# Conformer layer: six of eight convolution tiles on TensorE and two on VectorE, TensorE's order fixed from the second group of products on, two modulation vectors placed behind the convolution

## The chip, the core and the metric

One core of a Trainium2 chip runs the whole network in one launch. The metric is device time in microseconds (us), from the first to the last instruction with what the runtime adds around it; lower is better. The engines are TensorE (PE: matrix products; PEld is its weight load), VectorE (DVE), ScalarE (ACT), GpSimd (POOL), and SyncE (SP), whose queue issues nearly all DMA transfers, strictly in the order in which they stand there.

## The reference

Four layers over 256 latent tokens and 256 context tokens of 1024 features, in float32. Layers 0 and 3 mix tokens by attention, layer 1 by a Conformer convolution, layer 2 by a short convolution; each layer ends in an MLP. Every layer is modulated by six vectors, products of a conditioning vector with `mod_w[layer]` (1024 x 6144):

```python
def conformer_conv(h, w1, b1, dw, dwb, ln_g, ln_b, w2, b2):
    u = h @ w1 + b1
    a, g = jnp.split(u, 2, axis=-1)
    u = a * jax.nn.sigmoid(g)
    u = dwconv(u, dw) + dwb            # 31 taps along the tokens, each feature by itself
    u = jax.nn.silu(layernorm(u, ln_g, ln_b))
    return u @ w2 + b2

mod_l = (silu_c @ mod_w[i] + mod_b[i]).reshape(b, N_MOD, 1, D_MODEL)     # 0..5
a_l = modulate(rmsnorm(x, norm1_g[i]), mod_l[:, 0], mod_l[:, 1])
x = x + mod_l[:, 2] * y_l                                                # y_l: the mixer's output
m_l = modulate(rmsnorm(x, norm2_g[i]), mod_l[:, 3], mod_l[:, 4])
x = x + mod_l[:, 5] * sq_relu_mlp(m_l, mlp_w1[i], mlp_w2[i])
```

## The kernel before

Activations lie with features on the 128 partitions: eight tiles (j = 0 to 7) of 512 columns, 256 of the latent stream (s = 0) and 256 of the context (s = 1). A float32 product is three TensorE products of high and low halves (`mm3`, lines 105 to 107). Weights come by SP into four `raw` buffers (line 94, 512 KB each) and are split by ScalarE (line 221) and VectorE (line 222) into ten `w` buffers, five pairs.

**The Conformer** runs the first product `h @ w1` in four groups g, each giving tiles j = 2g and 2g+1: group 0 and group 3 by stream (`gemm_turns`, 256 columns at a time), groups 1 and 2 over 512 columns (`gemm`). VectorE forms the gated tile (`out`, line 1004). The 31 taps of a tile are then summed in one of two ways. `conv_vector` is a chain of 31 VectorE operations, handed out a few at a time by `run_some`. `conv_tensor` is 32 TensorE products for one stream or for both, four per tap group on four quarters of the columns of the array; the profile lists two records for each. It needs the tile written to DRAM and read back four times in shifted form (`shifted`, the `mem` and `u4` tiles, on SP) and a tile of tap weights built by VectorE (`tap_weights`). Before, VectorE has tiles 0, 1, 3 and the latent half of 5, and TensorE has 2, 4, 6, 7 and the other half of 5. `layer_norm(s)` follows for each stream: means by products with `ones_d`, squares, `rstd_newton`, `spread`, and the outputs `z`, which the second product (`cv_w2`, in `project`) reads.

**Modulation vectors** are made in two ways too. `mod_vectors` multiplies and adds on VectorE from 256 KB pieces (`mraw`, line 308); it is put in the background of a layer's MLP and steps at a given rate each time the MLP calls `tick`. `mod_tensor` makes a vector by 16 products on TensorE (line 371, two records each) from eight 512 KB pieces that pass through the same four `raw` buffers (issued at line 360), then a copy by ScalarE and four small products (line 380). `need(layer, m)` writes out what is missing of vector m at that place of the program.

**Order.** A scheduler places each engine's instructions by its own estimate, except where `manual_schedule` names an engine, whose instructions then stand as written. Before, this holds for TensorE in the block that begins at the first `self.need(layer, 3)` of `conformer`:

```python
with self.tc.manual_schedule(engines={mybir.EngineType.PE}):
    self.need(layer, 3)
    for j in (4, 6, 7):
        conv_tensor(j, slice(0, 1))
    lat = layer_norm(0)
    self.need(layer, 4)
    ...
```

The vectors of layer 1 are scheduled at line 1304 and after, in layer 0's MLP: 0 and 1, then 2, by `mod_vectors`; 3, 4 and 5 by `mod_tensor` at rate 0, so that they are made where `need` asks for them.

Of the kernel before, what the change touches and what calls it, by code (L numbers as in the profile page):

```python
# [13 lines left out]
ALU = mybir.AluOpType  # L14
# [5 lines left out]
LAT = 256  # L20
# [5 lines left out]
CONF_K = 31  # L26
CONF_PAD = 15
PITCH = 288
VECTOR_TILES = (0, 1, 3)
NEG = -1e30  # L30


class Net:
# [884 lines left out]
    def conformer(self, layer, slot, then):  # L918
        nc, t = self.nc, self.t
# [3 lines left out]
        conv = [None] * KT  # L923
        sig = {}
        two = lambda ap: ap.rearrange("p (s n) -> p s n", s=2)
        on_vector = []
        loaded = self.conv_taps(slot)
        next(loaded)

        def conv_vector(j, u, st):  # L930

            y = two(conv[j])[:, st]
            ys = [y, two(self.hid())[:, st] if j == 5 else y]
            tap = lambda i: self.par("cv_dw", i * KT + j)
            for i in range(CONF_K):
                if i == 0 or i == 1 and j == 5:
                    nc.vector.tensor_scalar(out=ys[i], in0=u[:, st, i:i + LAT], scalar1=tap(i),
                                            scalar2=None if i else self.par("cv_dwb", j), op0=ALU.mult,
                                            op1=ALU.bypass if i else ALU.add)
                else:  # L940
                    nc.vector.scalar_tensor_tensor(out=ys[i % 2], in0=u[:, st, i:i + LAT], scalar=tap(i), in1=ys[i % 2],  # L941
                                                   op0=ALU.mult, op1=ALU.add)
                yield 1
            if j == 5:
                nc.vector.tensor_tensor(out=y, in0=ys[0], in1=ys[1], op=ALU.add)

        def tap_weights(j):

# [33 lines left out]
        def run_some(n):  # L982

            while n and on_vector:
                g = on_vector.pop(0)
                if next(g, 0):
                    on_vector.append(g)
                    n -= 1

        u4, tapw, mem = {}, {}, {}  # L990
        glu = {}
        for g in range(4):
            def out(d, src, c, g=g):
# [13 lines left out]
                if j == 5:  # L1007
                    shifted(j, slice(1, 2))
                    conv[j] = self.hid()
                    on_vector.append(conv_vector(j, glu[j], slice(0, 1)))  # L1010
                    next(on_vector[-1])
                elif j not in VECTOR_TILES:
                    shifted(j, slice(c.start // LAT, c.stop // LAT))
                elif c.stop == NTOK:
                    conv[j] = self.hid()
                    on_vector.append(conv_vector(j, glu[j], slice(0, 2)))
                    next(on_vector[-1])
            segs = [(D + g * LAT, LAT), (g * LAT, LAT)]
            if g == 0:
                self.gemm_turns(self.chunk_pair(w1, segs), acts, out, first=True)  # L1020
            elif g < 3:
                for i, _ in enumerate(self.gemm(w1, segs, acts, cols, out)):
                    run_some(4)
                    if g == 1 and i == 1:
                        taps, mask = next(loaded)
                    if g == 1 and i == 4:
                        for j in (2, 4):
                            tapw[j] = tap_weights(j)
                    if g == 2 and i == 5:
                        conv[2] = self.hid()  # L1030
                        conv_tensor(2, slice(0, 2))
                        tapw[5] = tap_weights(5)
            else:
                self.gemm_turns(self.chunk_pair(w1, segs), acts, out)
                for j in (6, 7):
                    tapw[j] = tap_weights(j)
        for n, j in enumerate((4, 6, 7)):
# [9 lines left out]
        def layer_norm(s):  # L1047

            c = slice(s * LAT, (s + 1) * LAT)
            mean = self.ps()  # L1050
            added = [(4, 6), (4, 5, 6)][s]
            for j in added:
                nc.vector.tensor_tensor(out=total[:, c], in0=total[:, c], in1=conv[j][:, c], op=ALU.add)
            parts = [total] + [conv[j] for j in (4, 6, 7, 5) if j not in added]
            for n, part in enumerate(parts):
                nc.tensor.matmul(out=mean[:, :LAT], lhsT=self.ones_d, rhs=part[:, c], start=n == 0, stop=n == len(parts) - 1)
            for j in range(KT):
# [11 lines left out]
                self.split(y, z[k][0][:, c], z[k][1][:, c])  # L1069
            yield  # L1070

        with self.tc.manual_schedule(engines={mybir.EngineType.PE}):
            self.need(layer, 3)
            for j in (4, 6, 7):
                conv_tensor(j, slice(0, 1))
            lat = layer_norm(0)
            self.need(layer, 4)
            next(lat)
            for j in (4, 5):
                conv_tensor(j, slice(1, 2))  # L1080
# [204 lines left out]
    def run(self, out):  # L1285
# [5 lines left out]
        for layer in range(DEPTH):  # L1291
# [9 lines left out]
            else:  # L1301
                self.short_conv(layer, slot, mixer_end)
            if layer < DEPTH - 1:
                for vectors, rate in (([0, 1], 0.3), ([2], 0.3)) if layer == 0 else (([0, 1], 0.42), ([2], 0.42), ([3, 4], 0.42),
                                                                                   ([5], 0.25)):
# [46 lines left out]
```

## Time and profile before

| what | value |
|---|---|
| time, median of 3 runs | 2265.07 us (2263.01 to 2267.22) |
| the profiled execution's own time | 2267.25 us |
| its span, first to last instruction | 2265.5 us |
| TensorE busy | 2183.5 us (96%) |
| VectorE busy | 1529.6 us (68%) |
| mean granted TensorE clock | 0.982 of full speed |

Times inside the profile run from the span's start; the Conformer's stage lies at about 701 to 976 us. What lies around the span in the profiled execution is 2267.25 - 2265.5 = 1.75 us. Busy shares are means over stages that have different limits, so a change to one stage has to be read from that stage.

### The profile page before, as it was taken

What the parts mean: (1) busy time and instruction counts of PE and PEld (TensorE: products, weight loads), DVE (VectorE), ACT (ScalarE), POOL (GpSimd) and SP (SyncE); (2) the same over time, 40 slices, a digit from 0 to 9 for tenths busy, and PEclk for the clock granted to TensorE, in tenths of its full rate; (3) what the DMA queues carried; (4) which work ended last, traced back from release to release, by engine and by line L of the source; (5) the groups of instructions that cost most, each with busy time, mean ns of one, the idle gap of its engine ahead of it and who ended that gap; (6) DMA issues with size and microseconds to landing.
All of it is one profiled execution on the core that took longest, in us unless ns stands there. A gap on an engine that the chain in (4) does not pass through costs nothing.

```text
span 2265.5 us, 32711 instructions
## 1 busy us (share of the span) xinstructions
PE 2183.5 (96%) x12706; PEld 1789.6 (79%) x12706; DVE 1529.6 (68%) x2684; ACT 867.3 (38%) x1452; POOL 94.5 (4%) x167
## 2 busy tenths in 40 slices
PE   8999999999999848999999999999999999999998
PEld 5766678888889633888888898898888888778998
DVE  5365668585757962797777887579766557677665
ACT  4355544233233101652332332243323234666543
POOL 1112100000000000000000000000000000230000
PEclk9999999999999978999999999999999999999999
DMA  9565545453422255245455534325555425554653
GB/s 320 139 108 76 126 138 162 127 168 98 144 94 77 89 147 199 87 138 176 137 161 167 163 124 133 102 83 176 170 168 181 143 86 177 77 81 138 195 186 128
DMA packets 201308, 316.51 MB, mean 140 GB/s; under 512 B 13797, under 2 KB 68641, under 8 KB 201152
## 3 DMA queue, kind: packets, MB, share of 16 engines
q1 hardware_dynamic: 197232, 307.69, 43.1%
q0 software_dynamic: 3616, 6.60, 4.8%
q8 instruction: 100, 1.64, 0.3%
q14 instruction: 56, 0.46, 0.1%
q10 hardware_dynamic: 304, 0.12, 0.0%
HBM read 311.99 MB, written 2.38 MB: 139 GB/s over the span
## 4 chain that ended last, share of the span: by engine, by line
PE 89%; DVE 4%; issue 3%; DMA 3%; ACT 1%; POOL 0%; ACTq 0%; SPq 0%; POOLq 0%; DVEq 0%
PE mm L105 26%; PE mm L107 26%; PE mm L106 26%; PE mm L745 2%; PE x L735 2%; PE mm L978 2%; PE mm L707 1%; DVE h L941 1%; PE x L371 1%; PE mm L706 1%; DMA e<-in_na_rpb_dram 1%; DMA raw<-in_mod_w_dram 1%; DVE w L222 1%; DMA raw<-in_mlp_w_dram 0%; PE x L527 0%
## 5 line engine op out<-in xcount | busy, mean ns | idle before, releaser
L221 ACT ACTIVATE w<-raw 128x1024 fp32r<-128x1024 f32 (+1 forms) x377 | 392.7, 1054 | 672.1 <-PE mm L106 583.0
L222 DVE TENSOR_TENSOR w<-raw,w 128x1024 fp32r<-128x1024 f32 (+1 forms) x377 | 454.3, 1219 | 286.3 <-ACT w L221 285.2
L105 PE MATMUL mm<-a,w 128*128 128x512 f32 (+2 forms) x1792 | 630.5, 352 | 2.3 <-DVE t L629 1.4
L106 PE MATMUL mm<-a,w 128*128 128x512 f32 (+2 forms) x1792 | 627.3, 351 | 0.0
L107 PE MATMUL mm<-a,w 128*128 128x512 f32 (+2 forms) x1792 | 624.2, 350 | 1.1 <-DVE w L222 1.1
L106 PE MATMUL mm<-h,w 128*128 128x256 f32 (+1 forms) x1504 | 506.2, 337 | 0.4 <-DVE h L222 0.3
L105 PE MATMUL mm<-h,w 128*128 128x512 f32 (+1 forms) x1376 | 472.3, 343 | 0.0
L107 PE MATMUL mm<-h,w 128*128 128x512 f32 (+1 forms) x1376 | 469.8, 342 | 0.0
L105 PEld LDWEIGHTS mm<-a,w 128*128 128x128 f32 x1792 | 337.9, 189 | 54.0 <-issue 4.8
L107 PEld LDWEIGHTS mm<-a,w 128*128 128x128 f32 x1792 | 338.0, 189 | 51.0 <-DVE h L941 2.5
L106 PEld LDWEIGHTS mm<-a,w 128*128 128x128 f32 x1792 | 338.7, 189 | 45.7
L106 PEld LDWEIGHTS mm<-h,w 128*128 128x128 f32 x1504 | 283.8, 189 | 32.4 <-DVE h L222 0.8
L105 PEld LDWEIGHTS mm<-h,w 128*128 128x128 f32 x1376 | 259.0, 188 | 36.3 <-issue 3.9
L107 PEld LDWEIGHTS mm<-h,w 128*128 128x128 f32 x1376 | 259.0, 188 | 33.1 <-DVE mm L713 0.6
L316 DVE SCALAR_TENSOR_TENSOR macc<-mraw,cw,macc 128x512 f32<-128x512 f32 x364 | 255.1, 747 | 13.0 <-DMA mraw<-in_mod_w_dram 12.0
L588 DVE SCALAR_TENSOR_TENSOR x<-mm,mod,x 128x256 f32<-128x256 f32 x288 | 127.4, 479 | 97.8 <-PE mm L107 97.3
L221 ACT ACTIVATE h<-t 128x512 fp32r<-128x512 f32 (+1 forms) x148 | 81.0, 548 | 98.8 <-DVE t L619 85.6
L619 DVE SCALAR_TENSOR_TENSOR t<-mm,t 128x512 f32<-128x512 f32 (+1 forms) x136 | 79.3, 586 | 38.7 <-ACT t L618 38.3
L222 DVE TENSOR_TENSOR h<-t,h 128x512 fp32r<-128x512 f32 (+1 forms) x148 | 86.3, 583 | 25.1 <-ACT h L221 24.6
L618 ACT ACTIVATE t<-mm 128x512 f32<-128x512 f32 (+1 forms) x136 | 69.2, 511 | 85.8 <-PE mm L107 84.6
L371 PE MATMUL x<-raw,cw 128*32 128x512 f32 x224 | 44.8, 673 | 41.4 <-DMA raw<-in_mod_w_dram 41.3
L556 ACT ACTIVATE a<-t,mod 128x256 fp32r<-128x256 f32 x120 | 53.4, 501 | 59.3 <-DVE t L543 59.3
(177 smaller groups left out, 1834.7 us busy)
## 6 DMA issues: line engine op xcount, KB each, us to landing
raw<-in_mlp_w_dram SPq DMA_DIRECT2D x256, 512.0 KB
mraw<-in_mod_w_dram SPq DMA_DIRECT2D x240, 256.0 KB
raw<-in_mod_w_dram SPq DMA_DIRECT2D x56, 512.0 KB
raw<-in_na_wqkv_dram SPq DMA_DIRECT2D x64, 256.0 KB
raw<-in_sc_win_dram SPq DMA_DIRECT2D x24, 512.0 KB
h<-in_mod_w_dram SPq DMA_DIRECT2D x32, 256.0 KB
raw<-in_na_wqkv_dram SPq DMA_DIRECT2D x16, 512.0 KB
raw<-in_na_wo_dram SPq DMA_DIRECT2D x16, 512.0 KB
```

What stands on the lines that cost most here:

```text
L105: mm(out=out, lhsT=a[0], rhs=b[0], start=start, stop=False)
L106: mm(out=out, lhsT=a[0], rhs=b[1], start=False, stop=False)
L107: mm(out=out, lhsT=a[1], rhs=b[0], start=False, stop=stop)
L221: self.nc.scalar.activation(out=hi, in_=src, func=AF.Copy)
L222: self.nc.vector.tensor_tensor(out=lo, in0=src, in1=hi.bitcast(F32), op=ALU.subtract)
L316: nc.vector.scalar_tensor_tensor(out=acc[s], in0=raw, scalar=c, in1=acc[s], op0=ALU.mult, op1=ALU.add)
L371: nc.tensor.matmul(out=ps[32 * g:32 * g + 32], lhsT=self.cw[:, 4 * k0 + g, 2 - 2 * r:34 - 2 * r], rhs=tiles[g], start=n == 0, stop=n == 3, ...
L556: self.nc.scalar.activation(out=hi[:, c], in_=t, func=AF.Identity, bias=sh)
L588: self.nc.vector.scalar_tensor_tensor(out=x, in0=src[:, o:o + LAT], scalar=self.mod1(layer, m, s, j), in1=x, op0=ALU.mult, op1=ALU.add)
L618: nc.scalar.activation(out=r, in_=src, func=AF.Relu)
L619: nc.vector.scalar_tensor_tensor(out=h, in0=src, scalar=0.0, in1=r, op0=ALU.max, op1=ALU.mult)
L735: nc.tensor.transpose(out=tp[:, dst * P:(dst + 1) * P], in_=p[:, j * P:(j + 1) * P], identity=self.ident)
```

## The change

VectorE keeps tiles 0 and 1 whole. TensorE gets tiles 2 to 7 whole, each stream: tiles 2 and 3 before group 3, the others behind it. The means are one product for the VectorE-made total (tiles 0 to 3) and one for each of tiles 4 to 7. TensorE stands as written from the end of group 0 to the means of the second stream. Of layer 1's vectors, 0 to 3 are made by `mod_vectors` in layer 0's MLP (pairs at rate 0.55), and 4 and 5 by `mod_tensor` behind the second stream's means.

```diff
-VECTOR_TILES = (0, 1, 3)
+VECTOR_TILES = (0, 1)
...
+        in_order = ExitStack()
...
-                if j == 5:
-                    shifted(j, slice(1, 2))
-                    conv[j] = self.hid()
-                    on_vector.append(conv_vector(j, glu[j], slice(0, 1)))
-                    next(on_vector[-1])
-                elif j not in VECTOR_TILES:
+                if j not in VECTOR_TILES:
                     shifted(j, slice(c.start // LAT, c.stop // LAT))
...
             if g == 0:
                 self.gemm_turns(self.chunk_pair(w1, segs), acts, out, first=True)
+                in_order.enter_context(self.tc.manual_schedule(engines={mybir.EngineType.PE}))
             elif g < 3:
                 for i, _ in enumerate(self.gemm(w1, segs, acts, cols, out)):
-                    run_some(4)
+                    run_some(3)
                     if g == 1 and i == 1:
                         taps, mask = next(loaded)
-                    if g == 1 and i == 4:
-                        for j in (2, 4):
-                            tapw[j] = tap_weights(j)
-                    if g == 2 and i == 5:
-                        conv[2] = self.hid()
-                        conv_tensor(2, slice(0, 2))
-                        tapw[5] = tap_weights(5)
+                    if g == 2 and i in (2, 4):
+                        tapw[1 + i // 2] = tap_weights(1 + i // 2)
             else:
+                for j in (2, 3):
+                    conv[j] = self.hid()
+                    conv_tensor(j, slice(0, 2))
                 self.gemm_turns(self.chunk_pair(w1, segs), acts, out)
-                for j in (6, 7):
+                for j in (4, 5, 6, 7):
                     tapw[j] = tap_weights(j)
...
-            added = [(4, 6), (4, 5, 6)][s]
-            for j in added:
-                nc.vector.tensor_tensor(out=total[:, c], in0=total[:, c], in1=conv[j][:, c], op=ALU.add)
-            parts = [total] + [conv[j] for j in (4, 6, 7, 5) if j not in added]
+            parts = [total] + [conv[j] for j in (4, 5, 6, 7)]
...
-        with self.tc.manual_schedule(engines={mybir.EngineType.PE}):
-            self.need(layer, 3)
-            for j in (4, 6, 7):
+        with in_order:
+            for j in (4, 5, 6, 7):
                 conv_tensor(j, slice(0, 1))
             lat = layer_norm(0)
-            self.need(layer, 4)
             next(lat)
             for j in (4, 5):
                 conv_tensor(j, slice(1, 2))
-            self.need(layer, 5)
             next(lat)
             conv_tensor(6, slice(1, 2))
             next(lat)
             conv_tensor(7, slice(1, 2))
             other = layer_norm(1)
             next(other)
+            self.need(layer, 4, 5)
...
-                for vectors, rate in (([0, 1], 0.3), ([2], 0.3)) if layer == 0 else (...
+                for vectors, rate in (([0, 1], 0.55), ([2, 3], 0.55)) if layer == 0 else (...
...
-                    for m in (3, 4, 5):
+                    for m in (4, 5):
                         self.background(self.mod_tensor, 1, [m], 0.0)
```

On TensorE, behind the last product of group 3, there stood before all 16 products of vector 3 (line 371, out of `raw`), and the latent half of tile 4 (line 978) behind them:

```order
L107 MATMUL mm_7189<-a_6126,w_7029 128x256
L371 MATMUL x_7367<-raw_7368,cw 32x512 x2
L371 MATMUL x_7367<-raw_7370,cw 32x512 x2
L371 MATMUL x_7367<-raw_7376,cw 32x512 x2
L371 MATMUL x_7367<-raw_7378,cw 32x512 x2
L371 MATMUL x_7367<-raw_7384,cw 32x512 x2
L371 MATMUL x_7367<-raw_7386,cw 32x512 x2
L371 MATMUL x_7367<-raw_7392,cw 32x512 x2
L371 MATMUL x_7367<-raw_7394,cw 32x512 x2
L380 MATMUL x_7402<-mask_78,t_7400 128x4 x4
L978 MATMUL mm_7409<-u_1371_6958,tapw_6694 32x256
```

Now the latent half of tile 4 (line 975) stands at that place itself:

```order
L107 MATMUL mm_7291<-a_6206,w_7131 128x256
L975 MATMUL mm_7431<-u_1395_6995,tapw_7378 32x256
L975 MATMUL mm_7431<-u_1396_6996,tapw_7378 32x256
L975 MATMUL mm_7431<-u_1397_6997,tapw_7378 32x256
L975 MATMUL mm_7431<-u_1398_6998,tapw_7378 32x256
L975 MATMUL mm_7431<-u_1395_6995,tapw_7378 32x256
```

So the convolution no longer stands behind a vector's products on TensorE.

Before, TensorE had one product of tile 2's convolution (line 978) in the middle of group 2, with the low-half products of that group (line 107) behind it:

```order
L105 MATMUL mm_6835<-a_6112,w_6771 128x512
L106 MATMUL mm_6835<-a_6113,w_6771 128x512
L978 MATMUL mm_6903<-u_1341_6733,tapw_6690 32x512
L107 MATMUL mm_6784<-a_6112,w_6772 128x512
L105 MATMUL mm_6784<-a_6114,w_6771 128x512
```

Now tile 2's convolution begins behind the last product of group 2:

```order
L105 MATMUL mm_6910<-a_6206,w_6934 128x512
L106 MATMUL mm_6910<-a_6207,w_6934 128x512
L107 MATMUL mm_6910<-a_6206,w_6935 128x512
L975 MATMUL mm_7039<-u_1361_6801,tapw_6906 32x512
L975 MATMUL mm_7039<-u_1362_6802,tapw_6906 32x512
```

So no product of group 2 stands behind a product of the convolution any more.

On SP's queue, behind the last shifted reads (line 965), there now stand four pieces for layer 2's vectors (line 308), then twelve of the sixteen 512 KB pieces of vectors 4 and 5 (line 360), then the weights of the second product (line 94). The rows begin at the last shifted read, and the first six of the twelve pieces are shown:

```order
L965 DMA u_1436_7259<-mem_7260 128x1x263
L308 DMA mraw_8758<-in_mod_w_dram 128x512
L308 DMA mraw_8762<-in_mod_w_dram 128x512
L308 DMA mraw_8847<-in_mod_w_dram 128x512
L308 DMA mraw_8851<-in_mod_w_dram 128x512
L360 DMA raw_7864<-in_mod_w_dram 128x2x512
L360 DMA raw_7866<-in_mod_w_dram 128x2x512
L360 DMA raw_7872<-in_mod_w_dram 128x2x512
L360 DMA raw_7874<-in_mod_w_dram 128x2x512
L360 DMA raw_7891<-in_mod_w_dram 128x2x512
L360 DMA raw_7893<-in_mod_w_dram 128x2x512
```

Before, pieces of vector 3 (line 360) stood between the shifted reads (line 968) and writes (line 964):

```order
L964 DMA mem_6993<-u_6984 128x288
L360 DMA raw_7370<-in_mod_w_dram 128x2x512
L360 DMA raw_7376<-in_mod_w_dram 128x2x512
L968 DMA u_1377_6989<-mem_6993 128x1x263
L968 DMA u_1378_6990<-mem_6993 128x1x263
L968 DMA u_1379_6991<-mem_6993 128x1x263
L968 DMA u_1380_6992<-mem_6993 128x1x263
L360 DMA raw_7378<-in_mod_w_dram 128x2x512
L964 DMA mem_7144<-u_7136 128x288
```

So twelve pieces now stand together behind all shifted reads, and four, of vector 4, among them.

## Rows read from the trace of the kernel before

**Rows 1.** The page: span, and busy time, share and instructions of each engine.

```profile
span 2265.5 us, 32711 instructions
...
PE 2183.5 (96%) x12706; PEld 1789.6 (79%) x12706; DVE 1529.6 (68%) x2684; ACT 867.3 (38%) x1452; POOL 94.5 (4%) x167
```

**Rows 2.** Windows: stretch, length, each engine's busy us (records), granted clock, DMA share, GB/s.

```profile
749.00:757.00 8.00, 1.29 (x3) 0.18 (x2) 8.00 (x13) 0.00 (x0) 0.00 (x0) 0.82 0.21 60
...
810.00:857.00 47.00, 12.22 (x44) 3.00 (x38) 17.11 (x36) 0.59 (x1) 0.00 (x0) 0.59 0.55 157
...
869.00:911.00 42.00, 33.20 (x356) 14.71 (x349) 14.41 (x43) 12.96 (x24) 0.00 (x0) 0.92 0.77 255
...
929.00:966.00 37.00, 36.66 (x301) 36.48 (x301) 25.28 (x58) 25.85 (x52) 1.47 (x16) 0.97 0.24 72
```

**Rows 3.** Timeline, TensorE, groups 1 and 2: start, length, instruction, idle before and releaser.

```profile
724.60 0.39 PE L105 MATMUL mm<-a,w 128*128 128x512 f32 x1
724.84 0.39 PE L106 MATMUL mm<-a,w 128*128 128x512 f32 x1
...
755.72 1.89 PE L978 MATMUL mm<-u,tapw 128*32 128x512 f32 x2 [6.71 <-DMA u<-mem]
...
769.45 2.78 PE L978 MATMUL mm<-u,tapw 128*32 128x512 f32 x24
```

**Rows 4.** Timeline, TensorE, behind group 3.

```profile
809.72 1.91 PE L371 MATMUL x<-raw,cw 128*32 128x512 f32 x12
...
851.19 3.25 PE L371 MATMUL x<-raw,cw 128*32 128x512 f32 x8 [14.80 <-DMA raw<-in_mod_w_dram]
...
868.78 1.89 PE L371 MATMUL x<-raw,cw 128*32 128x512 f32 x16
873.81 5.05 PE L371 MATMUL x<-raw,cw 128*32 128x512 f32 x16 [3.15 <-DMA raw<-in_mod_w_dram]
879.55 1.06 PE L380 MATMUL x<-mask,t 128*128 128x4 f32 x8 [0.68 <-ACT t L376]
...
881.93 7.14 PE L978 MATMUL mm<-u,tapw 128*32 128x256 f32 x128
888.89 1.90 PE L371 MATMUL x<-raw,cw 128*32 128x512 f32 x16
...
902.28 3.66 PE L978 MATMUL mm<-u,tapw 128*32 128x256 f32 x64
905.87 0.71 PE L527 MATMUL x<-ident,s 128*128 128x128 f32 x4
```

**Rows 5.** Timeline, TensorE, between the two turns of the second product.

```profile
922.95 0.58 PE L490 MATMUL x<-ones,acc 128*128 128x1 f32 x4
925.84 1.19 PE L527 MATMUL x<-ident,s 128*128 128x128 f32 x4 [2.31 <-DVE s L519]
928.65 1.01 PE L105 MATMUL mm<-z,w 128*128 128x256 f32 x3 [1.62 <-ACT z L221]
```

**Rows 6.** Windows, TensorE alone, inside group 3.

```profile
791.00:809.00 18.00, 18.00 (x157) 1.00 0.48 135
```

**Rows 7.** Timeline, VectorE, in group 2.

```profile
754.83 1.22 DVE L222 TENSOR_TENSOR w<-raw,w 128x1024 fp32r<-128x1024 f32 x1
755.96 10.69 DVE L941 SCALAR_TENSOR_TENSOR h<-u,params,h 128x512 f32<-128x512 f32 x16
```

**Rows 8.** Timeline, SP's queue: shifted reads of tiles 6 and 7, one stream.

```profile
815.97 6.80 SPq L968 DMA_DIRECT2D u<-mem  x8
```

**Rows 9.** Windows: vectors' pieces alone on the DMA engines.

```profile
871.00:878.00 7.00, 4.13 (x14) 0.72 (x16) 0.00 (x0) 0.00 (x0) 0.00 (x0) 0.76 0.95 328
```

**Rows 10.** Windows: layer 0's MLP, and the next layer's.

```profile
340.00:473.00 133.00, 133.00 (x665) 112.77 (x666) 95.63 (x154) 45.92 (x71) 0.00 (x0) 0.98 0.47 148
...
1120.00:1160.00 40.00, 40.00 (x175) 32.47 (x174) 36.73 (x56) 8.50 (x8) 0.00 (x0) 1.00 0.60 185
```

**Rows 11.** Windows, line 316 alone (the multiply-adds of `mod_vectors`), on VectorE.

```profile
340.00:473.00 133.00, 27.35 (x40) 0.98 0.47 148
```

More of the change, by code (lines that the diff above doesn't have):

```diff
@@ L926, in conformer, with conv_vector @@
         on_vector = []
+        in_order = ExitStack()
         loaded = self.conv_taps(slot)
         next(loaded)
-        def conv_vector(j, u, st):
-            y = two(conv[j])[:, st]
-            ys = [y, two(self.hid())[:, st] if j == 5 else y]
+        def conv_vector(j, u):
+            y = two(conv[j])
             tap = lambda i: self.par("cv_dw", i * KT + j)
             for i in range(CONF_K):
[L936 to L939, printed above, removed]
+                if i == 0:
+                    nc.vector.tensor_scalar(out=y, in0=u[:, :, 0:LAT], scalar1=tap(0), scalar2=self.par("cv_dwb", j),
+                                            op0=ALU.mult, op1=ALU.add)
                 else:
-                    nc.vector.scalar_tensor_tensor(out=ys[i % 2], in0=u[:, st, i:i + LAT], scalar=tap(i), in1=ys[i % 2],
+                    nc.vector.scalar_tensor_tensor(out=y, in0=u[:, :, i:i + LAT], scalar=tap(i), in1=y,
                                                    op0=ALU.mult, op1=ALU.add)
                 yield 1
-            if j == 5:
-                nc.vector.tensor_tensor(out=y, in0=ys[0], in1=ys[1], op=ALU.add)
         def tap_weights(j):
@@ L1006, in out @@
                                                    op0=ALU.add, op1=ALU.mult)
-                if j == 5:
-                    shifted(j, slice(1, 2))
-                    conv[j] = self.hid()
-                    on_vector.append(conv_vector(j, glu[j], slice(0, 1)))
-                    next(on_vector[-1])
-                elif j not in VECTOR_TILES:
+                if j not in VECTOR_TILES:
                     shifted(j, slice(c.start // LAT, c.stop // LAT))
@@ L1015, in out @@
                     conv[j] = self.hid()
-                    on_vector.append(conv_vector(j, glu[j], slice(0, 2)))
+                    on_vector.append(conv_vector(j, glu[j]))
                     next(on_vector[-1])
@@ L1020, in conformer @@
                 self.gemm_turns(self.chunk_pair(w1, segs), acts, out, first=True)
+                in_order.enter_context(self.tc.manual_schedule(engines={mybir.EngineType.PE}))
             elif g < 3:
                 for i, _ in enumerate(self.gemm(w1, segs, acts, cols, out)):
-                    run_some(4)
+                    run_some(3)
                     if g == 1 and i == 1:
                         taps, mask = next(loaded)
-                    if g == 1 and i == 4:
-                        for j in (2, 4):
-                            tapw[j] = tap_weights(j)
-                    if g == 2 and i == 5:
-                        conv[2] = self.hid()
-                        conv_tensor(2, slice(0, 2))
-                        tapw[5] = tap_weights(5)
-            else:
+                    if g == 2 and i in (2, 4):
+                        tapw[1 + i // 2] = tap_weights(1 + i // 2)
+            else:
+                for j in (2, 3):
+                    conv[j] = self.hid()
+                    conv_tensor(j, slice(0, 2))
                 self.gemm_turns(self.chunk_pair(w1, segs), acts, out)
-                for j in (6, 7):
+                for j in (4, 5, 6, 7):
                     tapw[j] = tap_weights(j)
-        for n, j in enumerate((4, 6, 7)):
+        for n, j in enumerate((4, 5, 6, 7)):
             conv[j] = self.work.tile([P, NTOK], F32, tag=f"a{'hl'[n % 2]}{2 + n // 2}", name=self.name("conv"))
@@ L1303, in run @@
             if layer < DEPTH - 1:
-                for vectors, rate in (([0, 1], 0.3), ([2], 0.3)) if layer == 0 else (([0, 1], 0.42), ([2], 0.42), ([3, 4], 0.42),
+                for vectors, rate in (([0, 1], 0.55), ([2, 3], 0.55)) if layer == 0 else (([0, 1], 0.42), ([2], 0.42), ([3, 4], 0.42),
                                                                                    ([5], 0.25)):
```

## The prediction

> **What bounds the kernel now.** I read the page first: TensorE is busy 96% of the span and VectorE 68% [rows 1], so time can only come from work taken off TensorE or from stretches in which it stands still. The windows over the Conformer's stage show where it does: 1.29 of 8 us at 749 to 757, 12.22 of 47 at 810 to 857, 33.20 of 42 at 869 to 911 [rows 2]. The timeline of TensorE says for whom. At 749 to 755.72 it waits 6.71 us for a shifted read of tile 2 [rows 3]: the scheduler had put one product of that tile into the middle of group 2, and ready products of the group stood behind it. From 809.72 on it waits for pieces of `mod_w`: vector 3's last products start at 851.19 after an idle 14.80 and end at 854.44, and the convolutions that stand behind them had nothing to wait for but their place in the order. Vectors 4 and 5 repeat this at 868.78 and 888.89 in smaller form [rows 4]. Then the second product's two turns are parted by a chain of small VectorE operations (2.31 idle) and by the first `z` (1.62), so the second turn starts at 928.65 [rows 5]. VectorE is full where it matters least: 8.00 of 8 us at 749 to 757, but 17.11 of 47 at 810 to 857 [rows 2]. So this stage is bound by TensorE's order and by transfers, not by VectorE's taps.
>
> I time the changed stage from 724.60, where group 1 starts [rows 3], to the start of the second product's second turn, 928.65 before [rows 5]. Ahead of 724.60 only layer 0's background differs; behind 928.65 the same work follows.
>
> **Groups 1 to 3 and tiles 2 and 3.** Products of 512 columns start 0.235 apart [rows 3]; groups 1 and 2 have 192: 45.1, to 769.7. A convolution of both streams is 64 records, and 24 take 2.78 [rows 3], so 7.4; two take 14.8, to 784.5. This adds tile 3, 7.4, to TensorE. Group 3 has 192 products of 256 columns at 18/157 = 0.115 [rows 6]: 22.1, to 806.6. The wait of 6.71 has no successor here: tile 2's reads are asked for when its gated tile is written to DRAM, near 749 as before, and are first needed 20 us later.
>
> Does VectorE deliver in time? Group 2's second half needs two splits. In VectorE's new order 36 taps at 10.69/16 = 0.67 and three splits at 1.22 [rows 7] stand between 725.7 and them, and smaller operations that I put at 4 (an estimate): 32, so they end about 760, and TensorE wants them at 758.4. It loses 1 or 2 us, since the order is fixed. Group 3's splits stand two conv tiles ahead of their use and cost nothing; without tiles 2 and 3 in front of that group they would be 5 us late. I book 2 us for all this: 808.6.
>
> **The rest of the convolution.** Tiles 4 to 7 of the latent stream take 3.6 each (64 records, 902.28 to 905.87 [rows 4]): 14.4, to 823. The reads of tiles 6 and 7 (eight in 6.80 [rows 8]) are asked for behind the gated tiles, about 798, and TensorE reaches tile 6 at 816. The mean has five parts; three took 1.3 (880.6 to 881.93 [rows 4]), so 2.2, and 0.5 for ScalarE's copy of the last tile: 825.7. Tiles 4 and 5 of the context stream: 7.0 (881.93 to 888.89 [rows 4]). Sums 0.5, tile 6 3.6, spread 0.7, tile 7 3.6, means 2.7: 843.8. The taps that leave VectorE (31 of 0.67, and 31 of half the columns) are off the path on both sides; the half of tile 5 that TensorE gains, 3.6, is in the sum.
>
> **Vectors 4 and 5** now stand here with no convolution beside them. Four of sixteen pieces are in their buffers; the other twelve, 6.29 MB, can only be asked for as buffers come free, since there are four. Where this happened before, four pieces were freed from 868.78 to 870.67, and the four behind them were used up at 878.86 [rows 4]: 8.2. Three such rounds are 24.6. (Layer 2's four pieces ahead of them in the queue need the buffers of tap weights 4 and 5, free at about 833, so they hold nothing up.) While pieces alone were on the queues they moved at 328 GB/s [rows 9], and 12 x 0.524 MB at that is 19.2. In the second and third round two pieces are under way while two are used, so I take 22, and 19 to 25 for the range. The first four cost 1.9: last use at 867.7. The copy (0.68) and four small products (1.06) [rows 4]: 869.4. What was hidden before and is not now is this: 25.6 us of TensorE's path, where before all three vectors took about 45 + 12 + 13.
>
> [...]
>
> **The second product.** Its weights follow the pieces in the queue, and their first split falls into the chain behind the sums. The chain takes 2.9 (922.95 to 925.84 [rows 5]), with a split of 1.22 inside it 4.1; the spread 0.7: 874.2. Six products go ahead of it, 90 x 0.115 = 10.4 follow: 884.6. [...] The second turn no longer waits, because its stream's squares and chain are done. Against 928.65 this is 43.0, and the 1.1 that the second turn paid before is saved too: 44.
>
> **Layer 0's MLP** gets vector 3, 4 MB of pieces and 28 multiply-adds, and takes all four vectors at a higher rate. From 340 to 473 VectorE was busy 95.63 of 133 [rows 10], with 40 multiply-adds in 27.35, 0.68 each [rows 11]; the added ones with their first multiplies, turns and sums are about 26 us of VectorE in all. In the new order at most 60 multiply-adds lie in that stretch, so about 110 of 133, 83%. In layer 1's MLP VectorE was busy 36.73 of 40 with TensorE at 40.00 [rows 10]: the MLP's products hide such work. So nothing is the likeliest price, and 26 the highest if none of it is hidden; I take 1.
>
> Sum: 44 - 1 = 43. The profiled execution, 2267.25 (span 2265.5 and 1.75 around it), becomes 2224; it lay 2.2 above the median, so I predict **2222** for the median.
>
> **The rivals.**
> - *More is saved.* Pieces at 19.2, no late split, the chain hidden by weights that are late anyway: 3 + 2 + 2 more, 2215. Against it: four buffers only.
> - *Waits come up in the fixed order.* With TensorE's order fixed, one late read stops all. The 6.71 of rows 3 is what one costs. It could come at two of four places (tiles 2, 4, 6 latent, 6 context), since SP issues eight reads in 6.80 [rows 8] and each waits for its write: 13 less, 2235. The margins above, 8 to 20 us, speak against it. [...]
> - *VectorE becomes the bound in layer 0.* All 26 us show: 2247. For it, only that the work is uneven inside the 133 us; against it, the 92% of layer 1.
> - *Slower: the vectors' pieces come at the pace of vector 3.* Three of its pieces were used by 811.63 (12 records), the other five by 854.44: 8.6 each [rows 4]. Twelve at 8.6 are 103 instead of 22: 81 more, 2303. The gain is gone from 22 + 43 = 65, 5.4 a piece. For it: the same four buffers and the same queue. Against it: there SP stood between shifted writes and reads, and now the twelve stand behind all of them; the round at 870.67 had 2.05 a piece.
>
> **How the numbers follow.** No change in 0.2% (4.5 us) can be told. The sum holds with 0.64 (2214 to 2232: the stream's 19 to 25, the waits' 0 to 8), more with 0.08, the waits with 0.16 (2229 to 2241), layer 0 with 0.06, the pace with 0.06, of which 0.02 lies about no change. The range 2212 to 2240 leaves out the last two, the far tail of the waits and the edge of the first: under 0.2. Faster 0.94, same 0.02, slower 0.04.
>
> **What would show it.** Group 3's products should end near 808 with no idle of over 2 us behind 724.6; convolutions should run to about 843; then line 371 should show twelve pieces in 19 to 25 us, the one long wait of the stage. The second turn should start at about 886 without a wait. Layer 0's MLP should keep TensorE at its full rate. I am wrong if the convolutions wait for shifted reads, or if line 371 takes over 30 us.

## The result, and the profile after

The changed kernel takes **2233.24 us** (2231.26 to 2236.61) against 2264.2 for the kernel before (2263.01 to 2267.22): a ratio of 0.9863 [0.9849, 0.9878], 31 us or 1.4% faster. 2222 was forecast, with a range of 2212 to 2240. The profiled execution has a span of 2231.2 us, 34.3 less than that of before; the execution profiled before lay 3 us above its median. The page of the changed kernel, which answers to [rows 1]:

```profile
span 2231.2 us, 32928 instructions
...
PE 2188.0 (98%) x12804; PEld 1792.8 (80%) x12804; DVE 1522.8 (68%) x2656; ACT 865.7 (39%) x1453; POOL 94.7 (4%) x167
```

TensorE, which took over a tile and a half, is busy 4.5 us longer, and its share rises from 96% to 98%: so what went is time in which TensorE stood still. The windows of the changed kernel over the same stretches as [rows 2], and layer 0's MLP as in [rows 10]:

```profile
749.00:757.00 8.00, 8.00 (x36) 6.50 (x36) 8.00 (x14) 1.06 (x1) 0.00 (x0) 1.00 0.48 160
810.00:857.00 47.00, 39.18 (x508) 21.02 (x500) 13.48 (x43) 13.83 (x33) 0.00 (x0) 0.93 0.33 100
869.00:911.00 42.00, 36.43 (x242) 28.61 (x239) 21.26 (x47) 21.22 (x39) 0.00 (x0) 0.84 0.60 194
929.00:966.00 37.00, 36.04 (x275) 34.23 (x274) 33.49 (x78) 20.51 (x47) 0.74 (x8) 1.00 0.31 93
340.00:473.00 133.00, 132.98 (x674) 112.44 (x674) 111.74 (x181) 46.41 (x71) 0.00 (x0) 0.99 0.54 170
```

TensorE's first idle place, 749 to 757, is full, and the long one, 810 to 857, went from 12.22 busy us to 39.18. It still lacks 7.8 us there. TensorE's timeline behind group 2, the convolutions and the two vectors, which answers to [rows 4]:

```profile
769.03 7.93 PE L975 MATMUL mm<-u,tapw 128*32 128x512 f32 x70
777.51 7.06 PE L975 MATMUL mm<-u,tapw 128*32 128x512 f32 x58 [0.56 <-DMA u<-mem]
784.50 0.39 PE L105 MATMUL mm<-a,w 128*128 128x256 f32 x1
...
807.14 4.09 PE L975 MATMUL mm<-u,tapw 128*32 128x256 f32 x70
813.99 5.33 PE L975 MATMUL mm<-u,tapw 128*32 128x256 f32 x58 [2.77 <-DMA u<-mem]
820.53 0.59 PE L975 MATMUL mm<-u,tapw 128*32 128x256 f32 x2 [1.21 <-DMA u<-mem]
...
834.35 0.70 PE L1044 MATMUL mm<-total,ones_d 128*128 128x256 f32 x2
...
852.66 1.89 PE L1044 MATMUL mm<-conv,ones_d 128*128 128x256 f32 x8
854.48 1.92 PE L371 MATMUL x<-raw,cw 128*32 128x512 f32 x16
859.71 5.89 PE L371 MATMUL x<-raw,cw 128*32 128x512 f32 x16 [3.31 <-DMA raw<-in_mod_w_dram]
...
880.70 1.05 PE L380 MATMUL x<-mask,t 128*128 128x4 f32 x8 [0.74 <-ACT t L376]
881.62 0.59 PE L490 MATMUL x<-ones,acc 128*128 128x1 f32 x4
```

Groups 1 and 2 run without a stop from 724.33 to 769.1, and group 3 from 784.50 to 807.2. Then the four latent convolutions take from 807.14 to 834.35, **27.2 us where 14.4 were forecast**: six waits for shifted reads, 7.2 us in all (some of their rows are left out above), and between them products at a lower clock (granted 0.61 from 814 to 816 and 0.53 from 816 to 818, with 24 records in each of these stretches, where 808 to 810 has 44 at 1.00). From there on everything runs as in the forecast, 11 to 12 us late: the second means end at 854.55 instead of 843.8, the pieces of the vectors are used up at 879.96 instead of 867.7. The second product's two turns are no longer parted by a wait, and layer 1's MLP starts at 934.04, 31.5 us before the 965.50 of the kernel before.

SP's queue of the changed kernel over the same stretch, which answers to [rows 8]. The trace has the reads (L965) wait for their write (L961), 8.2 us of the 9.4 before 817.03, so the time from the one's issue to the other's holds the write's landing:

```profile
787.08 2.79 SPq L961 DMA_DIRECT2D mem<-u  x1
789.97 0.96 SPq L360 DMA_DIRECT2D raw<-in_mod_w_dram  x2
797.92 6.20 SPq L965 DMA_DIRECT2D u<-mem  x4
804.21 3.37 SPq L360 DMA_DIRECT2D raw<-in_mod_w_dram  x2
807.68 1.08 SPq L961 DMA_DIRECT2D mem<-u  x2
817.03 6.49 SPq L965 DMA_DIRECT2D u<-mem  x8
```

VectorE wrote the latent gated tiles 6 and 7 from 796.11 on; their write is issued only at 807.68, behind tile 5's reads and two pieces, and their reads only at 817.03, 9.4 us later. Tile 5's own reads, issued from 797.92 to 804.12, are not all there at 811.2, where the wait of 2.77 begins. So the question for the experiments is what makes this chain slow: the pieces among it, SP's queue, the trip through DRAM itself, or the reads.

### The profile page after: what moved, and what is told of

It is laid out like the page before. It is cut to its first block, busy times and chain, and to the rows that moved or that the text cites. A ratio compares the mean times of both kernels' runs of the same rounds, so it can differ in the third digit from the quotient of the medians.

```text
span 2231.2 us, 32928 instructions
## 1 busy us (share of the span) xinstructions
PE 2188.0 (98%) x12804; PEld 1792.8 (80%) x12804; DVE 1522.8 (68%) x2656; ACT 865.7 (39%) x1453; POOL 94.7 (4%) x167
## 4 chain that ended last, share of the span: by engine, by line
PE 91%; DMA 4%; DVE 3%; issue 1%; ACT 1%; POOL 0%; SPq 0%; ACTq 0%; POOLq 0%; DVEq 0%
PE mm L105 27%; PE mm L107 27%; PE mm L106 27%; PE mm L745 2%; PE x L735 2%; DMA u<-mem 2%; PE mm L707 1%; PE mm L975 1%; PE x L371 1%; PE mm L706 1%; DMA e<-in_na_rpb_dram 1%; DMA raw<-in_mod_w_dram 0%; DVE w L222 0%; DMA raw<-in_mlp_w_dram 0%; PE x L270 0%
## 5 line engine op out<-in xcount | busy, mean ns | idle before, releaser
L316 DVE SCALAR_TENSOR_TENSOR macc<-mraw,cw,macc 128x512 f32<-128x512 f32 x392 | 272.7, 750 | 11.1 <-DMA mraw<-in_mod_w_dram 10.3
L723 ACT ACTIVATE t<-mm,s 128x512 f32<-128x512 f32 (+1 forms) x96 | 58.9, 616 | 44.0 <-DVE s L721 43.2
```

The lines of the kernel that those rows point to most:

```text
L316: nc.vector.scalar_tensor_tensor(out=acc[s], in0=raw, scalar=c, in1=acc[s], op0=ALU.mult, op1=ALU.add)
L723: nc.scalar.activation(out=soft[:, g], in_=s[:, g], func=AF.Exp, bias=nm[:, i:i + 1], accum_out=sm[:, i:i + 1])
```

## The experiments

Each is compared with the kernel before, run beside it; the changed kernel's ratio is 0.9863.

**1. Six vectors early.** All six vectors of layer 1 go into layer 0's MLP; nothing of them is left in the Conformer.

```diff
-for vectors, rate in (([0, 1], 0.55), ([2, 3], 0.55)) if layer == 0 else ...
+for vectors, rate in (([0, 1], 0.62), ([2, 3], 0.62), ([4, 5], 0.62)) if layer == 0 else ...
...
-if layer == 0:
-    for m in (4, 5):
-        self.background(self.mod_tensor, 1, [m], 0.0)
```

> Changed kernel, but all six vectors of layer 1 are made by mod_vectors in layer 0's MLP (rate 0.62), none behind the convolution. Theory (the vectors' stream behind the convolution is a wait that nothing hides): from the second means to the second product the 25.5 us of line 371 and 2 x 1.8 us of copies and line 380 go, so the time falls from 2233 by about 27, to 2206; VectorE in layer 0's MLP rises from 84% to about 95% of 340 to 582 and TensorE there stays busy. Rival (VectorE becomes the bound of layer 0's MLP): the 52 us that two more vectors cost VectorE show there, layer 0's MLP ends 10 us or more later, and the time is 2216 or more. The shifted reads still stand in SP's queue, now with pieces of the second product's weights among them, so by the theory on reads (below) the second means still end near 850 to 858.

2212.1 us, ratio 0.976 [0.9747, 0.9773]: 21 to 23 us less than the changed kernel, so the stream of twelve pieces (25.5 us from 854.48 to 879.96) is nearly all on the path. It lies between the theory, 6 above it, and the rival. Two things are seen in its trace: TensorE is busy 131.04 of 133 us at 340 to 473 in layer 0 (VectorE 118.99), and the latent convolutions take 32.1 us where the changed kernel took 27.2. The first is not a price of the six vectors: with the same six, TensorE is busy 133.00 us there in experiment 5. Its own timeline of TensorE:

```profile
811.49 4.09 PE L975 MATMUL mm<-u,tapw 128*32 128x256 f32 x70
819.32 6.32 PE L975 MATMUL mm<-u,tapw 128*32 128x256 f32 x58 [3.74 <-DMA u<-mem]
...
843.46 0.70 PE L1044 MATMUL mm<-total,ones_d 128*128 128x256 f32 x2
```

Without a piece of vectors 4 and 5 in the stage, the reads are as late as with them. Pieces of `cv_w` stand among them in its queue instead.

**2. Vector 4's pieces held back** until the latent stream's last convolution, by a one-column copy on GpSimd into their buffers.

```diff
+                if layer == 1 and m == 4 and r == 0:
+                    nc.gpsimd.tensor_copy(out=raw[:, 0, 0:1], in_=self.held[:, LAT - 1:LAT])
...
+        self.held = conv[7]
```

> Changed kernel, but the first four pieces of vector 4 are held back by a one-column copy from tile 7's latent result, so they stand behind all shifted writes and reads in SP's queue instead of among them. Theory A (a shifted write lands late because pieces stand ahead of it or behind it on the same queue, SP stands still until it has landed, and so the reads of tiles 5 to 7 are late): tile 6's first read is issued near 805 to 808 instead of 817, TensorE waits 2 to 5 us less than the 12.8 us that the latent convolutions now take beyond their 14.4, the second means end at 845 to 849 instead of 854.5, and the time falls by 5 to 9, to 2224 to 2228. Theory B (the reads are slow by themselves, 1052-byte rows, whatever stands beside them): the second means end within 2 us of 854.5 and the time stays at 2231 to 2235.

2225.95 us, ratio 0.9821 [0.9808, 0.9835], in theory A's range: the first write of tiles 6 and 7 goes out 4.6 us sooner, and the latent convolutions take 20.8 us (808.90 to 829.72). But their reads are issued at 812.08, not by 808 as that theory has it, so the four pieces are only a part of it. SP's queue of this kernel, and its windows over the same time:

```profile
797.72 5.24 SPq L967 DMA_DIRECT2D u<-mem  x4
803.07 3.35 SPq L963 DMA_DIRECT2D mem<-u  x2
812.08 7.08 SPq L967 DMA_DIRECT2D u<-mem  x8
```

```profile
808.00:812.00 4.00, 4.00 (x69) 2.70 (x71) 0.88 (x2) 0.00 (x0) 0.00 (x0) 1.00 0.25 87
```

With no piece on the way it is still 9.0 us from the write's issue to that of its reads, and the DMA engines, which could move more (328 GB/s in [rows 9]), show a share of 0.25 and 87 GB/s meanwhile. The later theory starts from this row.

**3. Vector 3 alone.** The kernel before, with nothing of the change but vector 3 in layer 0 (two groups of vectors at 0.55, and no `need` for vector 3 in the Conformer).

> Kernel before, with one part of the change alone: vector 3 is made in layer 0's MLP (pairs at rate 0.55), vectors 4 and 5 stay where they were among the convolutions, tiles and TensorE's order as before. Theory (TensorE's wait for vector 3's pieces was the largest part of the loss): the 45 us from 809.7 to 855 shrink to the wait for the reads of tiles 6 and 7 and for VectorE's last taps at 826, so the latent convolutions end at 832 to 842 instead of 869 and the time falls by 25 to 32, to 2232 to 2239, that is nearly all of the whole change's 31. Rival (the tiles and the fixed order are what pays): the time falls by less than 12, to 2252 or more, since VectorE's taps end at 826 and the reads are as late as before.

2240.68 us, ratio 0.9885 [0.9872, 0.9899]: a gain of 25, a hair outside of what the theory expected and far from the rival. The first idle stays (5.84 us at 757.54), which in the changed kernel, with the fixed order and the new place of tile 2, is gone.

**4. Writes and reads on GpSimd's queue.** The shifted writes and reads (L961, L965) are issued with `nc.gpsimd.dma_start` in place of `nc.sync.dma_start`; the pieces stay on SP and stay early.

> Changed kernel, but the shifted writes and reads are issued by GpSimd's queue instead of SP's; the first four pieces of vector 4 stay early on SP's queue. Theory A (SP's single queue makes the reads late): writes land in under 4 us, all reads are there before TensorE wants them, the latent convolutions take 15 to 17 us instead of 27.2, the second means end near 844 and the time falls by 8 to 12, to 2221 to 2225. Theory B (the reads' own transfer is slow): the latent convolutions still take 23 us or more and the time stays at 2231 to 2235 or rises, should GpSimd issue them more slowly than SP does (6.2 us for four).

2220.76 us, ratio 0.9797 [0.9781, 0.9812]: theory A by the time, at the lower end of its range. TensorE's timeline of this kernel has the four convolutions in 14.2 us without a wait, as the forecast's 14.4:

```profile
809.19 14.16 PE L975 MATMUL mm<-u,tapw 128*32 128x256 f32 x256
823.28 0.70 PE L1044 MATMUL mm<-total,ones_d 128*128 128x256 f32 x2
```

The reason given in the expectation was wrong, though. On GpSimd's queue a write still lands late:

```profile
769.57 0.58 POOL L961 DMA_DIRECT2D mem<-u  x1 [4.37 <-DVE u L1001]
780.84 5.31 POOL L965 DMA_DIRECT2D u<-mem  x4 [10.69 <-DMA mem<-u]
...
799.91 1.14 POOL L961 DMA_DIRECT2D mem<-u  x2
808.73 5.44 POOL L965 DMA_DIRECT2D u<-mem  x8 [7.67 <-issue]
```

11.3 and 8.8 us from a write's issue to that of its reads. What got better is that the write of tiles 6 and 7 is issued at 799.91 instead of 807.68, and that the reads move faster once issued, with no piece on the way: 121 GB/s at a share of 0.63, against 96 and 0.27 in the changed kernel from 802 to 806. The windows of this kernel:

```profile
809.00:815.00 6.00, 6.00 (x111) 3.75 (x113) 0.88 (x2) 0.47 (x1) 5.75 (x9) 1.00 0.63 121
```

**5. Both: six vectors early, reads on GpSimd's queue.**

> The changed kernel with all six modulation vectors of layer 1 made in layer 0's MLP (as in the run with six vectors early) and the shifted writes and reads issued on GpSimd's queue (as in the run with the reads there). Theory: the two losses are separate, the stream of pieces behind the second means (25.5 us) and the latent convolutions' wait for their reads; with six vectors early the latent convolutions still took 32.1 us (811.49 to 843.54) where 14.4 is their bare length, because pieces of the weights stood among the reads. With the reads on their own queue 12 to 18 us of that go: 2194 to 2201. Rival: what the convolutions then save is lost again at the second product, whose weights are asked for at the same moments: 2206 or more.

2197.35 us, ratio 0.9696 [0.967, 0.9721], as expected by the time: the two gains, 21 and 12 us, add up. By the trace it is less clean: the latent convolutions take 21.4 us (808.62 to 830.05), with three waits for reads of 1.15 to 1.80, where experiment 4 had none.

**6. The vectors back among the convolutions.**

```diff
             lat = layer_norm(0)
+            self.need(layer, 4)
             next(lat)
             for j in (4, 5):
                 conv_tensor(j, slice(1, 2))
+            self.need(layer, 5)
...
-            self.need(layer, 4, 5)
```

> The changed kernel with vectors 4 and 5 put back among the convolutions in TensorE's order: vector 4 ahead of the latent stream's means, vector 5 behind tiles 4 and 5 of the context stream; all else as in the changed kernel. Theory: the stream of twelve pieces is bound by the four buffers and by transfers, so it is as long wherever it starts, and starting it 20 us earlier lets the 20 us of convolutions, means and sums lie beside it: 8 to 14 us faster than the changed kernel, 2219 to 2226. Rival (the prediction's step that nothing is lost by placing them behind, since ready convolutions otherwise stand behind waiting pieces): 2233 or more.

2242.74 us, ratio 0.9902 [0.9882, 0.9922]: 9 us slower than the changed kernel. My theory here fell, and the prediction's step holds. TensorE's timeline of this kernel:

```profile
834.03 1.88 PE L371 MATMUL x<-raw,cw 128*32 128x512 f32 x13
848.78 5.02 PE L371 MATMUL x<-raw,cw 128*32 128x512 f32 x16 [12.88 <-DMA raw<-in_mod_w_dram]
...
855.45 0.68 PE L1044 MATMUL mm<-total,ones_d 128*128 128x256 f32 x2
...
871.04 5.59 PE L371 MATMUL x<-raw,cw 128*32 128x512 f32 x16 [4.40 <-DMA raw<-in_mod_w_dram]
```

Ready convolutions stand behind 12.88 us of waiting. In this kernel the second round of pieces is asked for behind the context stream's eight reads (830.84 to 837.50 on SP's queue), so it starts late, and each vector pays its own first round.

**7. Tile 3 back on VectorE** (`VECTOR_TILES = (0, 1, 3)`, five tiles on TensorE; order and vectors as changed).

> The changed kernel with tile 3 back on VectorE (31 multiply-adds of 0.67 to 0.75 us, over both streams), so five tiles on TensorE; TensorE's order and the vectors stay as changed. Theory: behind group 3 the latent convolutions wait for shifted reads that come one tile after another, so the 7.5 us that TensorE saves ahead of group 3 are mostly waited away there: 2230 to 2236. Rival A: TensorE's own work bounds this stretch, and 7 us are saved: 2224 to 2228. Rival B: VectorE with 31 more multiply-adds is late with the splits and gated tiles: 2239 or more.

2222.61 us, ratio 0.9814 [0.9794, 0.9834]: about 11 us faster than the changed kernel. This is rival A and more; my theory, that the waits for reads would eat what TensorE saves, fell. Two things are saved by the trace: 7.1 us of TensorE's products, and one tile less in the chain of writes and reads, so that the latent write of tiles 6 and 7 is issued at 798.47 instead of 807.68. The latent convolutions' waits are then 2.33, put down to VectorE's multiply-adds, and 0.81, 0.81 and 0.41 for reads, in 24.0 us (800.72 to 824.73). So moving tile 3 to TensorE is a part of the change that costs time.

**8. No vector moved**: layer 0 as before (vectors 0 to 2 at 0.3), vectors 3, 4 and 5 behind the second means.

> The changed kernel without the change to layer 0: vectors 0, 1 and 2 there at the old rate 0.3, and vectors 3, 4 and 5 all three behind the second means in the Conformer. Tiles, order and reads as changed. Theory: eight pieces more in the stream at the 2.1 us a piece that it has in the changed kernel (25.5 for twelve), 17 us, and copy and products 1: 2249 to 2254. Rival A: what vector 3 alone gave to the kernel before, 24.8, is lost: 2256 to 2260. Rival B: part of its pieces come beside the convolutions, at no cost: under 2246.

2247.09 us, ratio 0.9921 [0.9902, 0.9941]: 13 to 14 us slower than the changed kernel, below the theory's 2249 and above rival B's bound. From the first start of line 371 to that of line 380 for the last vector it takes 40.2 us (855.81 to 896.01), and 26.2 in the changed kernel (854.48 to 880.70): the eight additional pieces cost 1.75 each, not 2.1. Without the vectors' move the rest of the change gives 18 us; vector 3's move gives 25 to the kernel before and 14 on top of the rest. These 18 hold the vectors' place (a gain of 9, experiment 6), tile 3's move (a loss of 11, experiment 7), and TensorE's fixed order with the new place of tile 2, which were not tried alone.

**9. The reads laid out anew.** A shifted read takes a block of 32 channels at four shifts, 128 rows of 1052 bytes for one stream. The source is walked with the 32 channels outermost instead of the four shifts; partitions change their order, and mask and tap weights follow.

```diff
-            n = len(range(2)[st])
-            for q in range(4):
-                src = mem[j][32 * q:32 * q + 32, st]
-                nc.sync.dma_start(out=u4[j][q][:, st, :LAT + 7], in_=bass.AP(
-                    src.tensor, src.offset, [[8, 4], [2 * PITCH, 32], [PITCH, n], [1, LAT + 7]]))
+            for s in range(2)[st]:
+                for q in range(4):
+                    src = mem[j][32 * q:32 * q + 32, s]
+                    nc.sync.dma_start(out=u4[j][q][:, s, :LAT + 7], in_=bass.AP(
+                        src.tensor, src.offset, [[2 * PITCH, 32], [8, 4], [1, LAT + 7]]))
...
```

> The changed kernel with the shifted reads laid out anew: the source is walked channel by channel (32, outermost) and shift by shift (4) in place of shift by shift and channel by channel, one read for each stream and quarter; mask and tap weights follow the new order of partitions. Issued on the same queue, the pieces stay early, the numbers are the same. Theory: the reads move on four of sixteen DMA engines (95 GB/s at a DMA share of 0.27 from 802 to 806), a tile's 1.05 MB takes 11 us, and the next tile's write lands only behind them, so the cause is the reads' own layout and neither the queue nor the pieces. Then the DMA share while reads move is over 0.5, writes land within 4 us, the latent convolutions run without waits of over 1 us (14 to 17 us instead of 27.2), and the time is 2218 to 2225. Rival A: a write and a read through DRAM take 7 to 9 us whatever their layout: 2229 or more, with the waits still there. Rival B: the pieces bound it, which share the queue: 2229 or more, with the share high and the waits there while pieces move.

2219.3 us, ratio 0.9793 [0.9778, 0.9808]: the theory, in each of its four numbers (share, landing, convolutions, time). First the changed kernel's windows, while tile 5's reads move and the next piece is only being asked for, then the same for this kernel, where reads move from 772 to 776 and from 812 to 816:

```profile
802.00:806.00 4.00, 4.00 (x37) 4.00 (x36) 0.98 (x2) 0.84 (x2) 0.00 (x0) 1.00 0.27 96
```

```profile
772.00:776.00 4.00, 4.00 (x44) 1.27 (x40) 4.00 (x5) 0.00 (x0) 0.00 (x0) 1.00 0.63 183
...
812.00:816.00 4.00, 4.00 (x80) 2.69 (x76) 0.00 (x0) 0.47 (x1) 0.00 (x0) 1.00 0.70 202
```

SP's queue and TensorE's timeline of this kernel:

```profile
796.24 0.81 SPq L963 DMA_DIRECT2D mem<-u  x2
798.03 5.35 SPq L967 DMA_DIRECT2D u<-mem  x8
```

```profile
806.72 14.04 PE L977 MATMUL mm<-u,tapw 128*32 128x256 f32 x256
820.69 0.70 PE L1046 MATMUL mm<-total,ones_d 128*128 128x256 f32 x2
```

The same queue, the pieces early, the same trip through DRAM: and the reads of tiles 6 and 7 are issued 1.8 us after their write, not 9.4, and the four convolutions run in 14.0 without a wait. So the cause was the reads' own layout. In the changed kernel the DMA share is 0.27 while they move, and a tile's 1.08 MB needs 11 us at 96 GB/s.

The traces also record every DMA packet with its start, length and size, and these show how the write is held. While tile 5's reads move alone, from 802 to 806 in the changed kernel, four or five of their rows are on the way at any moment; with the new layout, from 812 to 816, it is 11 in the median, and a row takes 47 ns in the median in both. An old read ends in 4 packets of 4 bytes, a new one in 16. And of the 256 rows of the write of tiles 6 and 7 in the changed kernel, 192 move from 811.43 to 813.19 and the last quarter, 64, only from 815.38 to 816.82, behind the last rows of tile 5's reads (813.43) and of the two pieces (816.10). With the pieces held back (experiment 2) the last quarter still waits for those reads (they end at 811.13, it moves from 810.89 to 811.85); with the new layout all 256 rows go from 797.08 to 798.06. So here the old reads held a quarter of what stood behind them, of the two pieces (whose rows split into 384 and 128) as of this write, and its reads were issued only at 817.03, behind its last quarter.

For the old reads 0.25 to 0.27 of 16 engines is an estimated 4.0 to 4.3 engines at work, which agrees with the four or five rows on the way and with the 4 packets at a read's end; how rows are divided over the engines is not shown, since no record here has the engines' numbers. The new reads' share of 0.63 to 0.70 goes with the time that SP needs to issue them: 0.135 MB every 0.67 us (eight in 5.35) is 201 GB/s, and the row from 812 to 816 has 202.

**10. Wide reads, and tile 3 on VectorE.**

> The kernel of the run with the wide reads, with tile 3 back on VectorE (five tiles on TensorE). Theory: of the 10.6 us that this gave to the changed kernel, 7.5 are the tile's own products on TensorE and about 3 the chain of reads, which is gone here: 6 to 9 us less than the wide reads alone, 2210 to 2218. Rival: VectorE's 31 multiply-adds are late with the sum of the convolutions once TensorE comes to it 10 us sooner: within 3 us of the wide reads alone.

2210.15 us, ratio 0.975 [0.9733, 0.9768]: 9 us less than the wide reads alone, at the upper edge. Counted from the start of group 1, the latent convolutions begin 74.8 us later instead of 81.2, so 6.4 of TensorE's 7.1 for the tile come off the path there, and the stretch of the vectors' pieces is 1.6 shorter; no row here shows the rest.

**11. This, with six vectors early.**

> The kernel of the run before it (wide reads, tile 3 on VectorE) with all six modulation vectors of layer 1 made in layer 0's MLP. Theory: the stream of pieces behind the second means goes, which gave 21 and 23 us in the two pairs of runs so far: 2188 to 2196. Rival: the second product's weights are not there when the convolutions end this soon, or layer 0's VectorE is late: 2198 or more.

2191.52 us, ratio 0.9669 [0.9655, 0.9684]: **the fastest of all, 42 us below the changed kernel and 75 below the one before**. The step from experiment 10 is 18.6, not 21 to 23, because VectorE's sum of its tiles is now late. The convolutions begin at the same moment as there (801.63 and 801.68), but with no piece ahead of them the second product's weights come sooner, and five of their splits (line 222, 1.22 each, one behind a wait of 1.62 for ScalarE) stand among VectorE's last multiply-adds: the sum's last step starts at 819.65 instead of 812.93. TensorE's timeline of this kernel:

```profile
801.63 14.04 PE L977 MATMUL mm<-u,tapw 128*32 128x256 f32 x256
820.49 1.19 PE L1046 MATMUL mm<-total,ones_d 128*128 128x256 f32 x2 [4.82 <-DVE total L1036]
```

## Why the prediction was right in its direction and too high in its gain

- **Stage start, groups 1 to 3, tiles 2 and 3** (to 808.6, 2 us of late splits included): right. Group 3 ended at 807.2, the 6.71 of [rows 3] has gone, and the largest wait in it is 0.56. The 2 us booked for late splits did not show; by the prediction's own terms (725.7 and 32) the splits end at 757.7, not at 760, ahead of the 758.4 at which TensorE wants them.
- **"The rest of the convolution"** (14.4 for tiles 4 to 7 of the latent stream): the step that failed. It took 27.2, and the second means ended 10.7 us late, against a miss of 11.2 in the time. The step set the time of the reads by when the gated tiles are written, "about 798", which was right (796.11), and added the issue of eight reads. It did not go through the queue: tile 5's reads and two pieces ahead of the write, 9.4 us from the write to its reads, and reads that move at a DMA share of about a quarter. The rows to price it stood in the trace of before and are shown below: the same write at 808.44 and its reads at 815.97 on SP's queue, and a DMA share of 0.22 at 67 GB/s from 816 to 823 while those eight reads moved. The rival "waits come up in the fixed order" named reads and SP's queue, at 2235 with a chance of 0.16: its mechanism is what happened, though the waits came one behind the other for tiles 5 to 7 of the latent stream and not at two of the four places that it named, and its time is the nearer one.
- **Vectors 4 and 5** (22, range 19 to 25, and 1.9): 25.5 with the first four, against 23.9, so the pace was right to 1.6 us, and the run with the vectors among the convolutions shows that to place them behind is worth 9 us even with nothing beside them.
- **The second product**: its chain had a wait of 2.39 for a split, as the 4.1 assumed, and the turns are not parted any more. No run shows the 1.1 that the sum books at the first turn and counts as saved at the second; in the changed kernel the granted clock was 0.50 from 882.8 to 889.5, where products start 0.21 apart instead of the 0.115 of [rows 6], and 1.00 from 890 to 934. As the 1.1 goes in and out, the 44 stands without it (928.65 - 884.6).
- **Layer 0** (VectorE at about 110 of 133, 83%, price 1): 111.74, 84%, and TensorE at 132.98, with 131.64 in the run with vector 3 alone: a price of 0 to 1.4, as booked. With six vectors there TensorE is busy 131.04, 133.00 and 131.90 us in the three runs, so no price beyond the spread of the runs is seen.
- **Not priced as a part**: that tile 3 moves to TensorE. The sum held its 7.4 on TensorE's path and never set them against VectorE, which in the changed kernel idles 28.62 us ahead of line 1046 at 836.81. Taken back alone, this part gives 11 us.

The rows of before on the step that failed, SP's queue and the windows while the reads move:

```profile
808.44 2.31 SPq L964 DMA_DIRECT2D mem<-u  x2
...
815.97 6.80 SPq L968 DMA_DIRECT2D u<-mem  x8
```

```profile
816.00:823.00 7.00, 1.47 (x4) 0.00 (x0) 7.00 (x15) 0.00 (x0) 0.00 (x0) 0.50 0.22 67
```

VectorE's wait in the changed kernel:

```profile
836.81 1.42 DVE L1046 TENSOR_TENSOR h<-h,mm 128x256 f32<-128x256 f32 x4 [28.62 <-PE mm L1044]
```

## What to carry to other kernels

A chain through memory (write, read back) is priced transfer by transfer along its queue: issue, what is ahead of it, landing, issue of the next; the time at which the producer is done says little (796.11 here, against 817.03 for the reads). A stretch in which transfers move alone at a DMA share that stays near a quarter was, here, a sign of their layout and not of the memory (0.27 with the old layout, 0.63 to 0.70 with the new): look at the outermost dimension of the pattern before moving work or queues. When several parts change at once, price each part against its own undoing: here two parts gained (the vectors' move and their place), and one, tile 3's move to TensorE, lost 11 us of that.

## What the runs showed of the hardware that was not expected

- Reads with four outermost rows moved at 96 GB/s and a DMA share of 0.27, with 32 outermost at 183 to 202 GB/s and 0.63 to 0.70; the reads behind a write of 0.29 MB (one tile in both streams, or two tiles in one) were issued 7.4 to 10.8 us after it in the changed kernel, and 1.8 to 3.1 us after it with the new layout, and of the write of tiles 6 and 7 the last quarter moved behind the old reads (815.38 to 816.82).
- The same narrow reads on GpSimd's queue reached a share of 0.63 at 121 GB/s. Why is not shown: no record here has the engines' numbers.
- After a wait of 2.77 us the granted clock of TensorE was 0.61 and 0.53 in the two next stretches of 2 us (814 to 818 in the changed kernel), so six short waits of 7.2 us went with 12.8 us lost in the latent convolutions.
